# Splitting weights by two DMAs from GpSimd in place of ScalarE and GpSimd arithmetic

## The chip, the cores and the metric

The kernel runs on one core of one Trainium2 chip. The metric is device time in microseconds for one execution of the whole program; for the kernel before, three runs gave 2639.9 to 2642.7 us with a median of 2642.7.

## The reference, cut to what matters

The reference is two transformer blocks with two layers each, on 512 tokens of width 1024, all in float32. What is computed, in the order of the program:

```python
h = h + dsa_attention(rms_norm(h, g_attn_a), w_in_a, w_o_a)   # layer A: top-128 keys by an index score
h = h + sq_relu_mlp(rms_norm(h, g_mlp[0]), w_up[0], w_down[0])
h = h + fox_attention(rms_norm(h, g_attn_b), w_q_b, w_o_b, *shared_kv(h, ...))   # layer B: causal, with decay
h = h + sq_relu_mlp(rms_norm(h, g_mlp[1]), w_up[1], w_down[1])
x = rms_norm(h, g_final)
x = x + g1 * gqa_attention(modulate(rmsnorm(x), sh1, sc1), ...)   # layer C: normed heads, not causal
x = x + g2 * sq_relu_mlp_2(modulate(rmsnorm(x), sh2, sc2), mlp_w_in[0], mlp_w_out[0])
x = x + g1 * chunked_gmlp(modulate(rmsnorm(x), sh1, sc1), ...)    # gated MLP, mixing tokens of a block
x = x + g2 * sq_relu_mlp_2(modulate(rmsnorm(x), sh2, sc2), mlp_w_in[1], mlp_w_out[1])
```

The modulation vectors (sh, sc, g) come from a small product of `ada_w` with a condition vector.

## The kernel before

The residual `h` stays in SBUF as eight tiles of 128 features by 512 tokens. TensorE multiplies in `float32r`, which does not carry all bits of a float32, so every operand is split in two: a high part, rounded to float32r, and a low part, the exact difference. A product is three matmuls (`mul3`: high by high, high by low, low by high). For a tile of 128 output features and 1024 input features that is 24 matmuls of 128x512.

A weight comes in by `weight`. SP issues a plain load of 512 KB to a buffer `wr` (two of them). ScalarE copies it to `wh` in float32r, which rounds it, and a subtraction writes `wl` (three buffers of each). In most of the program VectorE subtracts, on a whole tile. Where `self.low` names GpSimd, rounding and subtraction go by two halves of 512 columns and GpSimd subtracts. This is so in layer A but for the index key's weight and the second half of the output product, for the query weights of layer B, for the query weights from the fourth on in layer C, and in `first`.

`last` and `first` stand at the boundaries of stages. `last` makes the product that completes h; its last three tiles go by halves of the tokens, so that all three weights are held to the end, while the norm of the first half (`Norm.split`) runs beside the second half. `first` is the first three tiles of the next product by the same halves: 144 matmuls of 128x256. Four stages begin with it: layer C, the MLP behind it, the gated MLP, and the last MLP.

The order of instructions is not written by hand. The program is recorded by `Sched`; `order` plays it through with assumed durations (`cost`) and gives each engine the ready instruction of lowest number, and the engines then run their queues in that order, each waiting for what its next instruction needs. A DMA is assumed to hold its engine 60 ns, then to pass through one common queue. Names in the profile are tile names: `wr`, `wh`, `wl` for weights, `xh`, `xl` for the two parts of a normed input, `st` for stacked heads, `mask` for index scores and masks in layer A, `nb` and `rs` for the shift and the factor of a softmax row, `pr` for its probabilities, `rot` and `q` for rope. All instructions have the line of the helper that emits them, L413.

Of the kernel before, what the change touches and what calls it, by code (L numbers as in the profile page):

```python
# [18 lines left out]
P = 128          # partitions, tokens of a block, features of a tile  # L19
S = 512          # tokens  # L20
D = 1024
HALVES = slice(0, S // 2), slice(S // 2, S)
KD = D // P      # feature tiles of the model width
NB = S // P      # token blocks
# [7 lines left out]
# columns of the packed per-feature vectors  # L32
# [10 lines left out]
class View:  # L43
    """a part of a tile that is not placed yet; slices and reshapes are replayed on the real one"""
# [33 lines left out]
    def bitcast(self, *a):  # L78
        """to a type of the same size"""
        return View(self.tile, self.steps + (("bitcast", a, {}),), self.box, self.flat)  # L80
# [30 lines left out]
class VPool:  # L111
    def __init__(self, sched, name, bufs, space, before, below):
        self.sched, self.name, self.bufs, self.space = sched, name, bufs, space
        self.before = before      # pools whose room it takes over
        self.below = below
        self.left = 0             # operations not emitted yet
        self.shared = None
        self.open_ = None
        self.slots = {}
# [5 lines left out]
# ns from the end of an instruction to the start of one that needs it  # L125
# [28 lines left out]
class Sched:  # L154
    """Records the program, orders each engine's instructions by a list schedule
    (ready instruction of lowest number first), then emits them in that order."""
# [29 lines left out]
    def later(self, n):  # L186
        """instructions that give way to the next n of the program"""
# [5 lines left out]
    def after(self):  # L193
        """instructions that wait for the one before them"""
# [4 lines left out]
    def record(self, eng, name, args, kw):  # L199
# [17 lines left out]
        if name == "matmul":  # L217
            # the sums of a bank one after the other
# [23 lines left out]
    def cost(o, outs, ins):  # L242
        """ns that the engine is held, and ns until the result is there"""
        ps = any(x.tile.pool.space is not None for x in ins)
        if o.name == "dma_start":
            x = (outs + ins)[0]
            return 60, 1550 + (x.box[1] - x.box[0]) * x.size * 4 / 360
# [25 lines left out]
    def order(self):  # L273
# [7 lines left out]
        parked = []               # wait for pools to be shut  # L281
# [23 lines left out]
        def room(p, q):  # L305
            if not q["free"]:
                return False
            # the first slot of a tag is its own, the others are shared by all tags of the pool
# [12 lines left out]
        while ev:  # L321
# [11 lines left out]
            while again:  # L333
                again = False
                for e, heap in ready.items():
                    while heap and busy[e] <= now:
# [15 lines left out]
                        if e == "tensor":  # L352
                            # the array runs at half its clock for a while after a pause
# [13 lines left out]
                        for s in o.succs:  # L367
                            left[s.i] -= 1
                            s.wait = max(getattr(s, "wait", 0.0), done if e == "sync" else end + LATENCY.get((e, s.eng), 130))
# [50 lines left out]
class Norm:  # L420
    """h / rms(h) * gs + sh in two parts, by halves of the tokens; twice: of h / rms(h) * g_final"""
# [8 lines left out]
    def add(self, k, c=slice(0, S)):  # L430
        """the squares of a tile of h (times the gain) to their sums"""
# [5 lines left out]
        if half and c != self.part:  # L437
            # the squares of a half take turns in the halves of a tile
# [14 lines left out]
    def split(self, c):  # L453
# [10 lines left out]
        if self.twice:  # L464
            # 1/rms(h) / rms(h / rms(h) * g) = (mean((h g)^2) + eps (mean(h^2) + eps))^-1/2
# [24 lines left out]
class Net:  # L490
    def __init__(self, ctx, tc, I, out, stop=None):
# [3 lines left out]
        self.low = None  # L495
        pool = lambda name, **kw: ctx.enter_context(self.sched.tile_pool(name, **kw))
        self.pp = pool("pp", space=PSUM)
        self.pp.shared = 4        # and a bank for each of 4 tags
# [34 lines left out]
    def weight(self, src, n):  # L533
        """src: [128, n] in DRAM; returns its high and low part"""
        w = self.t(self.wp, "wr", [P, 1024], bufs=2)
        self.nc.sync.dma_start(w[:, :n], src)
        wh = self.t(self.wp, "wh", [P, 1024], F32R)
        wl = self.t(self.wp, "wl", [P, 1024], F32R)
        if self.low is None:
            self.split(wh[:, :n], wl[:, :n], w[:, :n])  # L540
        else:
            for f in (0, n // 2):
                c = slice(f, f + n // 2)
                self.split(wh[:, c], wl[:, c], w[:, c], self.low)
# [8 lines left out]
    def fm(self, src, xh, xl, w=None):  # L553
        """one tile of 128 output features, all tokens"""
# [8 lines left out]
    def tm(self, src, xh, xl, evac, banks=("mm", "mm", "lg", "tp")):  # L563
        """a strip of output features with the tokens on partitions; src: [u, 128, kk, n]"""
# [17 lines left out]
    def squares(self, col=None):  # L582
        """sums of the squares of h (times a gain) over the features: [token, 2 * block]"""
# [16 lines left out]
    def rms(self):  # L600
        """1/rms of the columns of h: [token, block], and spread over all partitions"""
# [35 lines left out]
    def last(self, src, xh, xl, gate, norm):  # L637
        """the product that completes h, and the norm of h; the end of both goes by halves of the tokens"""
# [20 lines left out]
    def first(self, src, xh, xl):  # L659
        """the first three tiles of a product, by halves of the tokens"""  # L660
        self.low = self.nc.gpsimd
        ws = [self.weight(s.rearrange("p k n -> p (k n)"), D) for s in src]
        self.low = None
# [40 lines left out]
    def rope(self, pool, ps, cos, sin, eng, n=P, q=None, ceng=None):  # L704
        """ps * cos + (its halves of each head exchanged) * sin, in SBUF; the first n rows, repeated"""
# [14 lines left out]
    def stacks(self, pool, tag, s, bufs=None):  # L720
        """for the two heads of s: [high; low] and [low; high] along the partitions"""
# [9 lines left out]
    def doubles(self, pool, tag, s, scale):  # L731
        """for the two heads of s, scaled: [high; high] and [low; low]"""
# [13 lines left out]
    def softmax(self, pool, npr, lhs, rhs, W, masks, extra, rows, on_act=False):  # L746
        """rows of probabilities of one head, block after block; W: block of queries to its number of keys;
        lhs, rhs: pairs of operands whose products add up to the logits; rows: a factor of each row of them;
        on_act: which engine divides by the sums"""
# [669 lines left out]
```

## Time and profile before

| what | value |
|---|---|
| timed runs | 2642.7, 2639.9, 2642.7 us |
| profiled execution, span from first to last instruction | 2640.9 us, 1.8 us under the median of the timed runs (no time of its own is given beside its span) |
| TensorE busy | 2570.4 us (97%) |
| VectorE, ScalarE, GpSimd busy | 1577.0, 1159.9, 467.8 us |
| moved by DMA | 292.39 MB, mean 111 GB/s |
| mean granted clock of TensorE | 0.990 |

Shares over the whole span are means over stages with different limits: 97% for TensorE says that little idle time is there to be had, and not in which stage. TensorE's busy time also holds what a matmul takes at half clock. Where stages are compared, the table by stretches of time is the one to read: for each stretch, the time that each engine was busy in it.

### The profile page before, as it was taken

The page shows a single profiled execution, that of the slowest core. Times are in us where ns is not written, and L with a number is a line of the kernel's source. Part 1 is how long each engine was busy: PE and PEld are TensorE (multiplying, and loading weights), DVE is VectorE, ACT ScalarE, POOL GpSimd, SP SyncE. Part 2 cuts the span into 40 slices and gives each one's busy share as a digit, 9 for nine tenths or more (in the row PEclk, how much of TensorE's full clock was granted, in tenths as well). Part 3 has the DMA queues.
Part 4 walks back from the last instruction along what each step waited for, and adds up shares of the span by engine and source line. Part 5 has one row for each costly group of instructions (what it writes and reads, how often), then busy time and mean ns, then how long its engine had stood idle before and what let it go on. Part 6 is the DMA issues. An engine that isn't in the chain of part 4 may idle for free.

```text
span 2640.9 us, 34588 instructions
## 1 busy us (share of the span) xinstructions
PE 2570.4 (97%) x12998; PEld 2173.2 (82%) x12998; DVE 1577.0 (60%) x2667; ACT 1159.9 (44%) x2096; POOL 467.8 (18%) x628
## 2 busy tenths in 40 slices
PE   8989998999999998999999999999999999999999
PEld 6769787888888886888876888888998888888887
DVE  7998875455468777435698544434546654644433
ACT  5678322334477423323687433323435443523322
POOL 3773000000075000000686200000202210200000
PEclk9999999999999999999999999999999999999999
DMA  4222784223231576222211132222333332222222
GB/s 148 87 69 84 253 263 142 96 88 108 88 89 57 190 253 210 98 99 84 96 47 35 65 110 98 96 96 88 99 108 120 103 100 90 87 103 96 96 97 95
DMA packets 92056, 292.39 MB, mean 111 GB/s; under 512 B 11760, under 2 KB 16112, under 8 KB 91888
## 3 DMA queue, kind: packets, MB, share of 16 engines
q1 hardware_dynamic: 91888, 290.18, 32.8%
q8 instruction: 102, 1.67, 0.2%
q14 instruction: 66, 0.54, 0.1%
HBM read 277.28 MB, written 2.10 MB: 106 GB/s over the span
## 4 chain that ended last, share of the span: by engine, by line
PE 75%; DVE 10%; DMA 8%; ACT 3%; issue 2%; POOL 2%; SPq 0%; DVEq 0%; ACTq 0%; POOLq 0%
PE mm L413 64%; DMA adaw<-in_ada_w 7%; PE lg L413 4%; PE tp L413 4%; PE po L413 3%; DVE ada L413 2%; DVE mask L413 1%; DVE st L413 1%; ACT pr L413 1%; DVE tl L413 1%; POOL pr L413 1%; DVE m L413 1%; DVE acc L413 1%; ACT st L413 1%; ACT th L413 1%
## 5 line engine op out<-in xcount | busy, mean ns | idle before, releaser
L413 ACT ACTIVATE wh<-wr 128x1024 fp32r<-128x1024 f32 (+2 forms) x480 | 449.0, 940 | 1047.1 <-PE mm L413 865.3
L413 PE MATMUL mm<-xh,wh 128*128 128x512 f32 (+1 forms) x1640 | 627.8, 384 | 7.4 <-ACT wh L413 7.2
L413 DVE TENSOR_TENSOR wl<-wr,wh 128x1024 fp32r<-128x1024 f32 (+1 forms) x382 | 452.4, 1185 | 303.2 <-ACT wh L413 297.1
L413 PE MATMUL mm<-xh,wl 128*128 128x512 f32 (+1 forms) x1640 | 627.2, 383 | 1.3 <-DVE wl L413 0.9
L413 PE MATMUL mm<-xl,wh 128*128 128x512 f32 (+1 forms) x1640 | 627.0, 383 | 0.6 <-POOL xl L413 0.4
L413 PE MATMUL mm<-ah,wh 128*128 128x512 f32 (+1 forms) x1072 | 409.4, 382 | 16.9 <-ACT ah L413 16.9
L413 PE MATMUL mm<-al,wh 128*128 128x512 f32 (+1 forms) x1072 | 409.9, 382 | 0.7 <-DVE al L413 0.7
L413 PE MATMUL mm<-ah,wl 128*128 128x512 f32 (+1 forms) x1072 | 408.8, 381 | 1.1 <-DVE wl L413 1.1
L413 PEld LDWEIGHTS mm<-xh,wh 128*128 128x128 f32 x1640 | 311.6, 190 | 61.5 <-ACT wh L413 7.2
L413 PEld LDWEIGHTS mm<-xh,wl 128*128 128x128 f32 x1640 | 312.0, 190 | 59.7 <-DVE wl L413 3.5
L413 PEld LDWEIGHTS mm<-xl,wh 128*128 128x128 f32 x1640 | 312.5, 191 | 55.7 <-POOL xl L413 1.2
L413 PEld LDWEIGHTS mm<-ah,wh 128*128 128x128 f32 x1072 | 202.6, 189 | 58.3 <-ACT ah L413 20.0
L413 PEld LDWEIGHTS mm<-al,wh 128*128 128x128 f32 x1072 | 202.6, 189 | 41.2 <-DVE al L413 3.0
L413 PEld LDWEIGHTS mm<-ah,wl 128*128 128x128 f32 x1072 | 202.8, 189 | 39.9 <-DVE wl L413 2.0
L413 DVE SCALAR_TENSOR_TENSOR h<-mm,mod,h 128x512 f32<-128x512 f32 (+1 forms) x113 | 79.7, 707 | 260.3 <-PE mm L413 260.2
L413 POOL TENSOR_TENSOR wl<-wr,wh 128x512 fp32r<-128x512 f32 x98 | 133.1, 1368 | 144.9 <-ACT wh L413 138.4
L413 DVE SCALAR_TENSOR_TENSOR ada<-adaw,cs,ada 128x512 f32<-128x512 f32 x168 | 119.0, 748 | 43.2 <-DMA adaw<-in_ada_w 42.4
L413 DVE TENSOR_TENSOR h<-mm,h 128x512 f32<-128x512 f32 (+1 forms) x91 | 56.5, 624 | 147.0 <-PE mm L413 147.0
L413 PE MATMUL tp<-ident,pr 128*128 128x128 f32 x576 | 115.0, 278 | 7.3 <-POOL pr L413 3.4
L413 POOL TENSOR_SCALAR pr<-pr,rs 128x512 f32<-128x512 f32 (+3 forms) x168 | 110.3, 667 | 48.4 <-DVE rs L413 34.5
L413 ACT ACTIVATE ah<-a 128x512 fp32r<-128x512 f32 x128 | 80.9, 632 | 83.7 <-DVE a L413 81.6
L413 POOL TENSOR_TENSOR r<-ms,mhalf 128x2 f32<-128x2 f32 (+1 forms) x10 | 9.3, 934 | 606.9 <-DVE ms L413 545.7
(259 smaller groups left out, 4087.6 us busy)
## 6 DMA issues: line engine op xcount, KB each, us to landing
adaw<-in_ada_w SPq DMA_DIRECT2D x96, 512.0 KB, 4.5
wr<-in_w_up SPq DMA_DIRECT2D x64, 512.0 KB, 3.5
wr<-in_w_down SPq DMA_DIRECT2D x64, 512.0 KB, 3.5
wr<-in_w_in SPq DMA_DIRECT2D x64, 512.0 KB, 3.4
wr<-in_w_out SPq DMA_DIRECT2D x64, 512.0 KB, 3.5
wr<-in_w_gu SPq DMA_DIRECT2D x24, 512.0 KB, 3.5
wr<-in_w_gv SPq DMA_DIRECT2D x32, 384.0 KB, 3.0
wr<-in_w_go SPq DMA_DIRECT2D x32, 384.0 KB, 2.9
```

Of the source, the lines that this page charges most:

```text
L413: getattr(getattr(self.nc, o.eng), o.name)(*args, **kw)
```

## The change

A weight that GpSimd helped to split is now made by two DMAs that GpSimd issues. The first goes from DRAM straight to `wh` and casts float32 to float32r. ScalarE then writes minus the high part to `wl`, on the whole tile. The second DMA reads the weight from DRAM again and adds it to `wl`. Neither `wr` nor a subtraction is left there. The flag `self.low` (an engine) becomes `self.by_dma`, set at the same places. In the scheduler a DMA on GpSimd is assumed to hold its engine for 1000 ns, and what waits for a DMA is released at its landing whichever engine issued it. Comments and docstrings are removed throughout, which moves line numbers and nothing else.

```diff
@@ def cost
         if o.name == "dma_start":
             x = (outs + ins)[0]
-            return 60, 1550 + (x.box[1] - x.box[0]) * x.size * 4 / 360
+            return 1000 if o.eng == "gpsimd" else 60, 1550 + (x.box[1] - x.box[0]) * x.size * 4 / 360
@@ def order
-                            s.wait = max(getattr(s, "wait", 0.0), done if e == "sync" else end + LATENCY.get((e, s.eng), 130))
+                            s.wait = max(getattr(s, "wait", 0.0), done if o.name == "dma_start" else end + LATENCY.get((e, s.eng), 130))
@@ def weight
+        nc = self.nc
+        if self.by_dma:
+            wh = self.t(self.wp, "wh", [P, 1024], F32R)
+            wl = self.t(self.wp, "wl", [P, 1024], F32R)
+            nc.gpsimd.dma_start(wh[:, :n], src)
+            nc.scalar.activation(wl[:, :n], wh[:, :n].bitcast(F32), AF.Copy, scale=-1.0)
+            nc.gpsimd.dma_start(wl[:, :n], src, accum_op=ALU.add)
+            return wh, wl
         w = self.t(self.wp, "wr", [P, 1024], bufs=2)
-        self.nc.sync.dma_start(w[:, :n], src)
+        nc.sync.dma_start(w[:, :n], src)
         wh = self.t(self.wp, "wh", [P, 1024], F32R)
         wl = self.t(self.wp, "wl", [P, 1024], F32R)
-        if self.low is None:
-            self.split(wh[:, :n], wl[:, :n], w[:, :n])
-        else:
-            for f in (0, n // 2):
-                c = slice(f, f + n // 2)
-                self.split(wh[:, c], wl[:, c], w[:, c], self.low)
+        self.split(wh[:, :n], wl[:, :n], w[:, :n])
         return wh, wl
@@ def first (and, in the same way, layer_a, layer_b, layer_c)
-        self.low = self.nc.gpsimd
+        self.by_dma = True
         ws = [self.weight(s.rearrange("p k n -> p (k n)"), D) for s in src]
-        self.low = None
+        self.by_dma = False
```

The list schedule moves with it. On TensorE, at the boundary into layer C, this stood before (`mm` is a sum in PSUM; the first two rows end the stage before, `ah` and `al` being its input):

```order
L413 MATMUL mm_11913<-al_11677,wh_11844 128x256
L413 MATMUL mm_11913<-ah_11672,wl_11860 128x256
L413 MATMUL mm_12093<-xh_2590_12016,wh_11987 128x256
L413 MATMUL mm_12093<-xl_2598_12028,wh_11987 128x256
L413 MATMUL mm_12093<-xh_2590_12016,wl_11998 128x256
L413 MATMUL mm_12104<-xh_2590_12016,wh_12047 128x256
L413 MATMUL mm_12104<-xl_2598_12028,wh_12047 128x256
L413 MATMUL mm_12104<-xh_2590_12016,wl_12061 128x256
```

And this stands there now (`po<-ones,acc` are the sums of squares for the second half's norm):

```order
L413 MATMUL mm_11817<-al_11581,wh_11748 128x256
L413 MATMUL mm_11817<-ah_11576,wl_11764 128x256
L413 MATMUL mm_11992<-xh_2558_11919,wh_11900 128x256
L413 MATMUL mm_11992<-xl_2566_11930,wh_11900 128x256
L413 MATMUL mm_12008<-xh_2558_11919,wh_11936 128x256
L413 MATMUL mm_12008<-xl_2566_11930,wh_11936 128x256
L413 MATMUL po_12036<-ones_78,acc_11607 128x2 x2
L413 MATMUL po_12036<-ones_78,acc_11613 128x2 x2
L413 MATMUL mm_11992<-xh_2558_11919,wl_11964 128x256
```

The first matmul on a low part comes third before; now four on high parts and the norm's sums come ahead of it, and the second tile's low part is wanted only after the whole first tile.

On GpSimd, at the same place, this stood before (`rf` and `r` are the norm's inverse roots, `xl` its low parts):

```order
L413 TENSOR_TENSOR rf_11976<-ms_11969,mhalf_84 128x2
L413 TENSOR_TENSOR r_11985<-m_2646_11974,mhalf_84 128x2
L413 TENSOR_TENSOR wl_11998<-wr_11826,wh_11987 128x512 x2
L413 TENSOR_TENSOR xl_2599_12050<-y_12007,xh_2591_12038 128x256
L413 TENSOR_TENSOR wl_12061<-wr_11875,wh_12047 128x512
L413 TENSOR_TENSOR xl_2601_12091<-y_12022,xh_2593_12071 128x256
L413 TENSOR_TENSOR wl_12061<-wr_11875,wh_12047 128x512
```

And this stands there now:

```order
L413 TENSOR_TENSOR rf_11880<-ms_11873,mhalf_84 128x2
L413 TENSOR_TENSOR r_11889<-m_2614_11878,mhalf_84 128x2
L413 DMA wh_11900<-in_w_k_c 128x1024
L413 DMA wh_11936<-in_w_k_c 128x1024
L413 TENSOR_TENSOR xl_2567_11954<-y_11911,xh_2559_11941 128x256
L413 TENSOR_TENSOR xl_2569_11968<-y_11923,xh_2561_11958 128x256
L413 MEMSET bd_11986 128x2
L413 DMA wl_11964<-in_w_k_c 128x1024
L413 DMA wh_12012<-in_w_q_c 128x1024
```

Each `wh` DMA waits for the slot that a weight of the stage before holds, and each `wl` DMA for ScalarE; the other low parts of the norm stand behind them.

On GpSimd in layer A, among the first heads' softmax (`nb`) and rope (`q`, `rot`), this stood before:

```order
L413 TENSOR_TENSOR q_922<-q_922,rot_932 128x512
L413 TENSOR_TENSOR wl_1008<-wr_919,wh_974 128x512
L413 TENSOR_TENSOR q_981<-q_981,cos_109 128x512
L413 TENSOR_TENSOR rot_989<-rot_989,sin_111 128x512
L413 TENSOR_TENSOR wl_1088<-wr_956,wh_1031 128x512
L413 TENSOR_SCALAR nb_1106<-mx_1085 128x1
```

And this stands there now:

```order
L413 DMA wh_1261<-in_w_q_a 128x1024
L413 TENSOR_TENSOR q_1097<-q_1097,rot_1108 128x512
L413 TENSOR_SCALAR nb_1312<-mx_1301 128x1 x2
L413 DMA wl_1304<-in_w_q_a 128x1024
L413 TENSOR_SCALAR nb_1343<-mx_1323 128x1 x2
L413 TENSOR_TENSOR q_1282<-q_1282,cos_109 128x512
```

Where a subtraction of half a tile stood among softmax and rope, a DMA now stands, with its own wait.

## Rows read from the trace of the kernel before

**Rows 1.** Page, part 1: busy us, share of span, instructions.

```profile
PE 2570.4 (97%) x12998; PEld 2173.2 (82%) x12998; DVE 1577.0 (60%) x2667; ACT 1159.9 (44%) x2096; POOL 467.8 (18%) x628
```

**Rows 2.** By stretch: length, busy time of each engine, granted clock, DMA share, GB/s.

```profile
33.00:231.00 198.00, 178.70 (x1040) 147.84 (x1039) 189.10 (x534) 142.32 (x391) 127.99 (x174) 0.97 0.23 72
726.00:858.00 132.00, 129.73 (x751) 110.57 (x751) 100.59 (x319) 99.60 (x280) 85.23 (x158) 1.00 0.25 73
1290.00:1455.00 165.00, 155.90 (x844) 121.09 (x843) 142.26 (x268) 129.50 (x273) 126.11 (x163) 1.00 0.17 52
409.00:419.00 10.00, 5.63 (x12) 3.35 (x12) 8.89 (x12) 2.99 (x4) 0.00 (x0) 0.50 0.58 197
```

**Rows 3.** GpSimd's groups, 13 to 231 us: busy us, mean ns, idle before.

```profile
L413 POOL TENSOR_TENSOR wl<-wr,wh 128x512 fp32r<-128x512 f32 x46 | 64.0, 1402 | 51.5 <-ACT wh L413 49.8 <-PE lg L413 1.5
L413 POOL TENSOR_TENSOR q<-q,rot 128x512 f32<-128x512 f32 x10 | 13.5, 1345 | 2.0 <-DVE q L413 2.0
...
L413 POOL TENSOR_TENSOR rot<-rot,sin 128x512 f32<-128x512 f32 x10 | 13.0, 1304 | 1.7 <-DMA rot<-q 1.7
L413 POOL TENSOR_TENSOR q<-q,cos 128x512 f32<-128x512 f32 x8 | 11.2, 1406 | 4.0 <-DMA rot<-q 4.0
```

**Rows 4.** VectorE's groups, 13 to 231 us, one shape each.

```profile
L413 DVE TENSOR_TENSOR st<-q,st 64x512 fp32r<-64x512 f32 x16 | 21.2, 1326 | 0.8 <-ACT st L413 0.2
...
L413 DVE SCALAR_TENSOR_TENSOR mask<-rl,wi,mask 128x512 f32<-128x512 f32 x7 | 7.0, 1002 | 0.1
...
L413 DVE TENSOR_TENSOR st<-st,rot 128x512 f32<-128x512 f32 x5 | 5.6, 1119 | 0.1
...
L413 DVE TENSOR_TENSOR rot<-rot,sin 128x512 f32<-128x512 f32 x5 | 3.4, 680 | 0.0
...
L413 DVE SCALAR_TENSOR_TENSOR kdl<-q,kdh 64x512 fp32r<-64x512 f32 x4 | 2.7, 679 | 0.1
...
L413 DVE SCALAR_TENSOR_TENSOR xl<-h,vec,xh 128x512 fp32r<-128x512 f32 x1 | 0.7, 743 | 0.0
```

**Rows 5.** Instructions in time, boundary into layer C: start, us, [idle before].

```profile
1256.62 1.15 ACT L413 ACTIVATE wh<-wr 128x512 fp32r<-128x512 f32 x2 [2.48 <-PE mm L413]
...
1262.49 0.28 PE L413 MATMUL mm<-xh,wh 128*128 128x256 f32 x1
1262.61 0.28 PE L413 MATMUL mm<-xl,wh 128*128 128x256 f32 x1
...
1269.38 1.01 PE L413 MATMUL po<-ones,acc 128*128 128x2 f32 x4 [2.32 <-DVE acc L413]
...
1286.83 0.28 PE L413 MATMUL mm<-xh,wl 128*128 128x256 f32 x1
```

**Rows 6.** The same, first and last matmul of the three other boundaries.

```profile
1499.09 0.28 PE L413 MATMUL mm<-xh,wh 128*128 128x256 f32 x1
...
1519.98 0.28 PE L413 MATMUL mm<-xh,wl 128*128 128x256 f32 x1
...
1853.56 0.28 PE L413 MATMUL mm<-xh,wh 128*128 128x256 f32 x1
...
1874.46 0.28 PE L413 MATMUL mm<-xh,wl 128*128 128x256 f32 x1
...
2284.94 0.29 PE L413 MATMUL mm<-xh,wh 128*128 128x256 f32 x1
...
2304.60 0.28 PE L413 MATMUL mm<-xh,wl 128*128 128x256 f32 x1
```

**Rows 7.** A DMA issue on SP's queue, in time.

```profile
1.16 0.42 SPq L413 DMA_DIRECT2D wr<-in_w_ki  x1
```

**Rows 8.** DMA issues: count, KB each, median us to landing.

```profile
wr<-in_w_up SPq DMA_DIRECT2D x64, 512.0 KB, 3.5
...
wr<-in_w_gv SPq DMA_DIRECT2D x32, 384.0 KB, 3.0
...
h<-in_x SPq DMA_DIRECT2D x8, 256.0 KB, 5.2
```

More of the change, by code (lines that the diff above doesn't have):

```diff
@@ L659, in first @@
     def first(self, src, xh, xl):
-        self.low = self.nc.gpsimd
+        self.by_dma = True
         ws = [self.weight(s.rearrange("p k n -> p (k n)"), D) for s in src]
-        self.low = None
+        self.by_dma = False
         ps = [self.mm() for _ in src]
@@ L852, in layer_a @@
         kw = self.fm(I["w_ki"], xh, xl, first)
-        self.low = nc.gpsimd
+        self.by_dma = True
         r, rb = self.rms()
@@ L945, in layer_a @@
                     attend(ap, j, o1[j], 4, 3, (2, 3), False)
-                self.low = None
+                self.by_dma = False
                 self.half_out(w, o1, HALVES[1])
@@ L1017, in layer_b @@
                         with self.sched.later(50 if j else 0):
-                            self.low = nc.gpsimd
+                            self.by_dma = True
                             ps = self.fm(I["w_q_b"][j], xh, xl)
-                            self.low = None
+                            self.by_dma = False
                             s = self.t(pool, "s", [P, S])
@@ L1102, in layer_c @@
                     with self.sched.later(200 if j > 1 else 0):
-                        self.low = nc.gpsimd if j > 2 else None
+                        self.by_dma = j > 2
                         ps = q0 if j == 0 else self.fm(I["w_q_c"][j], xh, xl)
-                        self.low = None
+                        self.by_dma = False
                         s = self.rope(pool, ps, tab["q", 0], tab["q", 1], nc.gpsimd if j else nc.vector)
```

## The prediction

> **What bounds the kernel now.** I read first the page's busy shares, then busy time by stretch, then who is slowed inside the attention layers, and last the boundaries between stages. TensorE is busy for 97% of the span [rows 1], so nearly all the time is matmuls that the change leaves alone; what can move is the idle time of TensorE and the stages that another engine holds up. The table by stretches shows where those are. From 33 to 231 us (layer A) TensorE is busy 178.7 of 198 us, so 19.3 us are idle, and VectorE, busy 189.1, is the bound. In layer B (726 to 858 us) TensorE has 2.3 us idle, so next to nothing is to be had there. In layer C (1290 to 1455 us) it has 9.1 us idle of 165, with all of VectorE, ScalarE and GpSimd busy for over three quarters [rows 2].
>
> Inside layer A the reader should compare durations of one shape. The 46 `wl` subtractions take 64.0 us of GpSimd; with its three rope groups (13.5, 13.0, 11.2 us), which also read two tiles from SBUF, that makes 101.7 us, of which `wl` is 63% [rows 3]. VectorE instructions with two SBUF operands run longer here than the same work elsewhere: `st<-q,st` takes 1326 ns against 679 for `kdl<-q,kdh` of the same 64x512, `mask` 1002 against 743 for `xl`, `st<-st,rot` 1119 against 680 for `rot<-rot,sin` [rows 4]. The excess is 16 x 0.647 + 7 x 0.259 + 5 x 0.439 = 14.4 us. I put 63% of it, 9.1 us, down to the subtractions that go.
>
> At the boundaries, four of which use `first`, the weights' high and low parts live in three slots each, and the last three products of the stage before hold all of them. The first slot comes free at 1256.62, when ScalarE's wait for TensorE ends. The first matmul of layer C is at 1262.49, so the slot is free 5.9 us ahead; the 144 matmuls of `first` stand 0.12 us apart and end at 1286.95 [rows 5]. That is 17.3 us of work in 24.5 us; the rest is a wait of 2.3 us and half clock. The three other boundaries take 21.0, 21.0 and 19.8 us [rows 6]; the four together 86.3.
>
> **The change part by part.** 49 weights (24 in layer A, 8 in B, 8 in C, 9 in the three later `first`) change their way. Each loses a load on SP, two ScalarE roundings of half a tile and two GpSimd subtractions of 1.40 us, and gains a casting DMA, one ScalarE copy of the whole tile times -1, and an accumulating DMA, both issued by GpSimd.
>
> *Prices that this trace does not show.* No DMA is issued by GpSimd here, so three costs need bounds. Issue on GpSimd: not under 0.42 us, what SP's queue spends [rows 7], and I cap it at the 1.40 us of the subtraction that it replaces; the scheduler's new line assumes 1.0, which lies in the middle, and I take that. Landing of a plain 512 KB load is 3.5 us, of 384 KB 3.0 [rows 8]: 0.5 us for each 128 KB, so 2.0 us that go with size and 1.5 that do not. The cast moves the same bytes: 3.5 at best, 5.5 if its size part doubles; I take 3.5. The accumulation also has to read its destination: 3.5 at best, 5.5 with a doubled and 9.5 with a fourfold size part; I take 5.5. The copy times -1 is taken as the two half roundings in the trace, 1.15 us [rows 5].
>
> The Trainium skill ("DMA: Bandwidth & Descriptors", section "Anatomy of one DMA — SWDGE (gpsimd) path") gives a DMA from GpSimd 2.0 us plus its bytes at 436 GB/s, which for 512 KB is an estimate of 3.2 us, and makes no extra charge for accumulation. No row here shows it; by it the two landings would add up to 6.4 us instead of 9.0, and the sum would be near the first rival's.
>
> *The four boundaries.* Before, the load waited in a buffer of its own, and only rounding and subtraction had to wait for the slot. Now the load itself does. From a slot's release the chain is 1.0 + 3.5 + 1.15 + 1.0 + 5.5 = 12.2 us, so the first low part is there 12.2 - 5.9 = 6.3 us after the stage's first matmul could start. The order on TensorE has only four matmuls on high parts and the norm's sums ahead of the first that needs `wl`, so it waits. Then 140 matmuls remain, 16.8 us. The second and third slot come free 2.9 us apart (24 x 0.12), as fast as a half tile is used up, so I add no further wait. A pause of this length lowers the clock: from 409 to 419 us, with 4.4 us idle, the granted clock was 0.50 (1.2 GHz) and the 5.6 us of work there would have taken half at 2.4 GHz, 2.8 us lost [rows 2]; I take 2.5. That makes 6.3 + 16.8 + 2.5 = 25.6 us each, 102.4 in all, **16.1 us more** than 86.3. Part of the second half's norm ends sooner, as VectorE has no subtraction beside it, but it is not what the first low part waits for.
>
> *Layer A.* The 9.1 us of VectorE come back where it bounds, with TensorE's 19.3 us of idle time as the cap. Against it: GpSimd's and ScalarE's queues are in order, so `wl`'s DMA waits on GpSimd for ScalarE's copy, and that one on ScalarE for the first landing; behind them stand `nb` and rope, for which ScalarE's exponentials and the score products wait. I count **8 us gained**, within 0 and 13.
>
> *Layer C.* 5 weights free 10 x 1.40 us of GpSimd and spend 10 x 1.0 on issue: 4 us of an engine that is one of three in the way. **1 us gained.** *Layer B:* 2.3 us of idle time at most, **nothing**. *ScalarE:* two halves become one tile, no more than 0.2 us each, off the path. *SP* loses 49 issues and was not waited for.
>
> *The start.* Two casting loads of 512 KB go out at once beside the eight loads of h, which land after 5.2 us [rows 8]; before, the w_qi loads stood behind them in SP's queue. h later by 0 to 3 us, the time of 1 MB at 0.5 us for 128 KB being 4: **1 us lost**.
>
> Sum: 16.1 - 8 - 1 + 1 = +8.1 us, a span of 2649.0. The profiled span of 2640.9 lies 1.8 us below the median of the timed runs, 2642.7, so I predict **2651 us**.
>
> **The rivals.** *First: the two DMAs are as quick as a plain load, and the end is faster.* Issue 0.42, landing 3.5 each: the chain is 9.0 us, the first low part comes 3.1 us late, a boundary takes 3.1 + 16.8 + 1 = 20.9 us, 2.7 us less than before over the four. Layer A then gains 12, as queues do not hold up each other and VectorE's other stretched forms, too, find an emptier GpSimd, and layer C 4: -19 us, 2624. For it: with 5.9 us ahead, a chain of up to about 10 us costs a boundary nothing, since it has 4 us of slack of its own. Against it: nothing in the trace reads a destination and writes it at a plain load's speed. The mechanism decides where both landings together fall under about 7.5 us.
>
> *Second: the accumulation is far slower, and the in-order queues hand the delay on.* Issue 1.4, cast 5.5, accumulation 9.5: the chain is 19.0 us, a boundary 13.1 + 16.8 + 2.5 = 32.4, 129.6 in all or 43 more. A slot's round of 19.0 us and 24 matmuls at 0.24 makes 8.2 us for each weight with three slots, close to the 9.6 us that layer A has for each of its 24 (231 us), so its gain turns into some 12 us lost; start and layer B add 3 each: +61, 2704. Against it: DMA engines are idle for three quarters of layer A (share 0.23, [rows 2]).
>
> *Third: nothing moves*, since layer A's gain and the boundaries' loss cancel: 2643. It is the near end of the forecast and not a mechanism of its own.
>
> **How the numbers follow.** Forecast 0.47, spread from 2641 to 2665; first rival 0.28; second 0.25. What a measurement of this kernel can tell from no change is 0.2%, 5.3 us. Faster than 2637.4: nearly all of the first rival, 0.27. Within: the near end of the forecast and a bit of the first rival, 0.18. Slower than 2648: 0.55. The range leaves about a tenth on each side: 2628 to 2695; the forecast's own is 2641 to 2665.
>
> **What would show it.** Right: at each boundary TensorE waits 5 to 7 us for `wl` behind the first four matmuls on `xh`, followed by half clock; the `wl` DMAs land 5 to 6 us after issue, the `wh` ones after 3 to 4; in layer A `st<-q,st` falls from 1326 ns towards 900 and TensorE's idle time shrinks. The boundary step is wrong if `first` ends in under 22 us. Layer A's step is wrong if VectorE's durations fall and the stage does not get shorter, with GpSimd waiting at its DMAs for ScalarE or for slots. The prediction falls as a whole if landings lie outside 3 to 7 us, or if issuing holds GpSimd much longer than 1.4 us.

## The result and the profile after

The changed kernel takes 2706.9 us (median of 4 runs, 2704.1 to 2710.0) against 2641.3 us for the kernel before on the same chip (median of 4): 1.025 times as long, 95% interval 1.0234 to 1.0267. The profiled execution spans 2705.2 us, 64.3 more than before. I had predicted 2651 us within 2628 to 2695: the right sign, an eighth of the size, and outside the range. The second rival's 2704 was the nearest number.

The page's busy shares answer to [rows 1]. TensorE is busy 22 us longer with the same 12998 matmuls, while the mean granted clock falls from 0.990 to 0.978; GpSimd and VectorE are busy 66 and 24 us less.

```profile
PE 2592.3 (96%) x12998; PEld 2195.1 (81%) x12998; DVE 1553.4 (57%) x2667; ACT 1157.8 (43%) x2047; POOL 402.1 (15%) x628
```

I split the span at the first sums of squares of each norm (`po<-ones,acc`), which TensorE does in both kernels. The stretches of the changed kernel, in order, from the start through layer A, the first MLP, layer B, its MLP and layer C, up to the second MLP's norm (columns as in [rows 2]):

```profile
0.00:24.90 24.90, 12.78 (x34) 8.81 (x34) 12.29 (x19) 15.73 (x24) 4.27 (x13) 0.93 0.88 276
24.90:293.30 268.40, 239.17 (x1409) 205.99 (x1407) 212.89 (x600) 169.53 (x417) 106.79 (x179) 0.92 0.52 123
293.30:660.60 367.30, 358.69 (x1603) 294.48 (x1602) 219.07 (x287) 115.79 (x148) 2.02 (x2) 0.99 0.49 158
660.60:920.40 259.80, 253.72 (x1451) 218.48 (x1450) 164.93 (x412) 157.94 (x362) 79.00 (x161) 1.00 0.39 105
920.40:1282.00 361.60, 351.58 (x1595) 290.47 (x1594) 213.54 (x282) 112.04 (x142) 1.48 (x1) 0.98 0.49 160
1282.00:1536.10 254.10, 230.69 (x1299) 190.02 (x1298) 182.26 (x339) 163.28 (x329) 133.56 (x191) 0.95 0.27 69
```

The same stretches of before, split alike, are 21.2, 248.9, 369.2, 255.2, 360.0 and 237.3 us; layer A and layer C among them:

```profile
21.20:270.10 248.90, 229.21 (x1397) 195.32 (x1398) 227.22 (x599) 171.95 (x441) 137.63 (x182) 0.97 0.28 91
1254.50:1491.80 237.30, 225.81 (x1298) 185.17 (x1297) 183.26 (x339) 163.09 (x337) 147.69 (x191) 0.99 0.19 61
```

Beside my terms:

| term | predicted | measured |
|---|---|---|
| start | +1 | +3.7 |
| layer A | -8 | +19.4 |
| layer B | 0 | +4.6 |
| layer C without its boundary | -1 | +14.9 |
| the four boundaries | +16.1 | +22.2 |
| all the rest | 0 | -0.5 |
| sum | +8.1 | +64.3 |

The table is the reading that matters: the boundaries came out about as worked out, and the attention layers, which I had down as a gain, lost 39 us.

**The prices.** Medians from issue to landing over the whole run, columns as in [rows 8]:

```profile
wh<-in_w_q_a POOLq DMA_DIRECT2D x8, 512.0 KB, 4.4
wl<-in_w_q_a POOLq DMA_DIRECT2D x8, 512.0 KB, 5.6
...
wh<-in_w_in POOLq DMA_DIRECT2D x6, 512.0 KB, 3.9
wl<-in_w_in POOLq DMA_DIRECT2D x6, 512.0 KB, 8.0
wh<-in_w_qi POOLq DMA_DIRECT2D x4, 512.0 KB, 6.5
h<-in_x SPq DMA_DIRECT2D x8, 256.0 KB, 7.3
```

Accumulations land 5.4 to 5.7 us after issue in the layers (5.5 predicted), and casts 3.7 to 6.5 (3.5 predicted). Those of `w_in`, at the second and the last boundary, have a median of 8.0. The packet records say why casts scatter. GpSimd's DMAs go through one queue, in order. A cast issued while the queue is empty (17 of 49) has its first packet 1.3 us later and its last 3.5 us after issue; one issued while an accumulation runs (21 of 49) has its first packet 4.05 us after issue and its last 5.7. A 4 KB packet takes 174 ns when it casts and 328 ns when it accumulates. By the Trainium skill ("DMA: Bandwidth & Descriptors", "Anatomy of one DMA — SWDGE (gpsimd) path") the estimate is 3.2 us, with no price of its own for an accumulation. That is near the 3.5 us of a cast alone and does not hold for an accumulation, whose last packet comes 5.1 us after issue when the queue is empty; the measurement decides. The Trainium skill ("DMA: Bandwidth & Descriptors", "SWDGE vs HWDGE vs iDMA") says that only one such queue is allocated; the trace agrees, with 4.05 us against 1.3 to the first packet.

**A boundary.** Into layer C, GpSimd, ScalarE and TensorE in time (start, us, idle before), answering to [rows 5]:

```profile
1284.62 0.64 POOL L413 DMA_DIRECT2D wh<-in_w_k_c  x1 [0.28 <-issue]
...
1288.48 1.04 ACT L413 ACTIVATE wl<-wh 128x1024 fp32r<-128x1024 f32 x1
...
1289.83 0.91 POOL L413 DMA_DIRECT2D wl<-in_w_k_c  x1
...
1289.98 0.28 PE L413 MATMUL mm<-xh,wh 128*128 128x256 f32 x1
...
1291.40 0.39 PE L413 MATMUL mm<-xh,wh 128*128 128x256 f32 x1 [1.02 <-DMA wh<-in_w_k_c]
...
1294.12 0.82 PE L413 MATMUL po<-ones,acc 128*128 128x2 f32 x4 [2.21 <-DVE acc L413]
1295.19 1.01 PE L413 MATMUL po<-ones,acc 128*128 128x2 f32 x4 [0.25 <-DVE ms L413]
1296.07 0.56 PE L413 MATMUL mm<-xh,wl 128*128 128x256 f32 x1
...
1316.19 0.28 PE L413 MATMUL mm<-xh,wl 128*128 128x256 f32 x1
```

The cast goes out at 1284.62, the copy ends at 1289.52, the accumulation goes out at 1289.83 and lands 5.5 us later, at 1295.30: 10.7 us after the cast's issue (12.2 predicted), 5.3 us behind the stage's first matmul (6.3 predicted). TensorE uses it at 1296.07, 6.1 us behind that matmul. It does not stand still for the low part here: it waits 1.0 us for the second high part and 2.2 us for VectorE's sums of the norm, which stand ahead of the low part in its order, and their matmuls last past the landing. At the three other boundaries the wait for `wl` is there, 4.0, 4.5 and 4.0 us, after 1.0 to 1.6 us for a high part; the second one:

```profile
1544.76 0.39 PE L413 MATMUL mm<-xh,wh 128*128 128x256 f32 x1 [1.00 <-DMA wh<-in_w_in]
...
1549.22 0.58 PE L413 MATMUL mm<-xh,wl 128*128 128x256 f32 x1 [3.96 <-DMA wl<-in_w_in]
```

The low parts there are used 5.9, 6.6 and 9.4 us behind the first matmul. Into layer C the matmuls behind it are 0.21 us apart instead of 0.12 for a while; from 1295 to 1316 us the granted clock is 0.85. From the first to the last of the 144 matmuls, 0.12 us added as before, the four boundaries take 26.3, 26.4, 26.7 and 29.0 us, 108.4 against 86.3 [rows 5, 6].

**Inside layer A.** What TensorE waits for from 13 to 294 us (in total, times, longest):

```profile
PE lg L413 <- DVE st L413: 10.2, 8, 3.5
PE mm L413 <- DMA wl<-in_w_q_a: 7.0, 3, 5.1
PE mm L413 <- DMA wl<-in_w_qi: 4.7, 1, 4.7
PE tp L413 <- ACT pr L413: 4.0, 4, 2.1
PE po L413 <- ACT th L413: 2.9, 3, 2.2
PE mm L413 <- DMA wl<-in_w_o_a: 1.4, 1, 1.4
```

Three of the six are late low parts, 13.1 us, and none of these stood in the trace before. VectorE's relief is there, as the 46 subtractions of [rows 3] are gone: `st<-q,st` fell from 1326 ns [rows 4] to 1041, `mask<-rl,wi,mask` of 512 columns from 1002 to 748, and VectorE, busy for 227 of the layer's 249 us before, is busy for 213 of 268: it no longer bounds it. Idle time is only half of the layer's loss: by the two rows of the layer above, TensorE is idle for 29.2 us (19.7 before) and busy for 10.0 us more with nearly as many matmuls, at a granted clock of 0.92 against 0.97. One of the waits, in time:

```profile
101.53 0.85 POOL L413 DMA_DIRECT2D wl<-in_w_q_a  x1 [6.73 <-ACT wl L413]
102.37 0.58 POOL L413 DMA_DIRECT2D wh<-in_w_q_a  x1
106.48 0.56 POOL L413 DMA_DIRECT2D wh<-in_w_q_a  x1 [3.53 <-PE mm L413]
...
110.43 1.07 ACT L413 ACTIVATE wl<-wh 128x1024 fp32r<-128x1024 f32 x1 [3.35 <-DMA wh<-in_w_q_a]
...
110.68 1.29 POOL L413 TENSOR_TENSOR q<-q,cos 128x512 f32<-128x512 f32 x1 [3.65 <-DMA rot<-q]
...
113.17 0.89 POOL L413 DMA_DIRECT2D wl<-in_w_q_a  x1
...
118.71 0.79 PE L413 MATMUL mm<-xh,wl 128*128 128x512 f32 x1 [5.07 <-DMA wl<-in_w_q_a]
```

The cast issued at 102.37 stands in the DMA queue behind the accumulation of 101.53, so ScalarE's copy starts only at 110.43, 8.1 us after the cast's issue. GpSimd has by then begun rope, which waited 3.65 us for its own small transfers (`rot<-q`, 64 KB, lands after 3.4 us here, 2.0 before), and issues the accumulation behind it at 113.17. TensorE stands still for 5.07 us.

### The profile page after: what moved, and what is told of

It is laid out like the page before. It is cut to its first block, busy times and chain, and to the rows that moved or that the text cites. A ratio compares the mean times of both kernels' runs of the same rounds, so it can differ in the third digit from the quotient of the medians.

```text
span 2705.2 us, 34567 instructions
## 1 busy us (share of the span) xinstructions
PE 2592.3 (96%) x12998; PEld 2195.1 (81%) x12998; DVE 1553.4 (57%) x2667; ACT 1157.8 (43%) x2047; POOL 402.1 (15%) x628
## 4 chain that ended last, share of the span: by engine, by line
PE 72%; DMA 12%; DVE 7%; ACT 4%; issue 4%; POOL 1%; SPq 1%; DVEq 0%; POOLq 0%; ACTq 0%
PE mm L413 63%; DMA adaw<-in_ada_w 6%; PE lg L413 4%; PE tp L413 3%; PE po L413 2%; DVE ada L413 2%; DMA rot<-q 1%; ACT pr L413 1%; DVE st L413 1%; DMA wl<-in_w_in 1%; SPq L413 1%; DVE wl L413 1%; DVE tl L413 1%; ACT th L413 1%; DMA wl<-in_w_q_a 0%
## 5 line engine op out<-in xcount | busy, mean ns | idle before, releaser
L413 ACT ACTIVATE wh<-wr 128x1024 fp32r<-128x1024 f32 (+1 forms) x382 | 389.5, 1020 | 1035.2 <-PE mm L413 870.1
L413 PEld LDWEIGHTS mm<-ah,wh 128*128 128x128 f32 x1072 | 203.2, 190 | 58.4 <-ACT ah L413 19.8
L413 DVE TENSOR_TENSOR al<-a,ah 128x512 fp32r<-128x512 f32 x128 | 88.2, 691 | 46.5 <-ACT ah L413 46.4
L413 DVE TENSOR_TENSOR tl<-tp,th 128x512 fp32r<-128x512 f32 (+1 forms) x224 | 103.5, 493 | 13.9 <-ACT th L413 12.4
```

Of the source, the lines that this page charges most:

```text
L413: getattr(getattr(self.nc, o.eng), o.name)(*args, **kw)
```

## The experiments

All were run against the kernel before on the same chip; ratios are to it. Stage times are from one trace each, split as above. Where the instructions of layer A stand in the same order, its length still differs between traces: 265.1, 268.4 and 268.9 us (e2, the change, e3), 253.7 and 259.2 (e9, e13), 247.7 to 249.0 (e1, before, e14). So a stage's difference of less than some 5 us is not told from chance. The ways of `weight` were made selectable for each of its four places (`first`, A, B, C); "old" is the way before.

**e1: `first` alone.**

```diff
+WAYS = {"first": "dma", "A": "old", "B": "old", "C": "old"}
```

> The two DMAs only where a stage starts with first (12 weights in layer C, the two MLPs and the gated one); the 37 other weights of layers A, B and C as before. All theories agree that the four boundaries alone come out: they took 109.2 us after against 86.3 before, so some 2664 us (before + 23). If the waits of the attention layers had come from the boundaries (a later start that shifts their order), it would be nearer 2690.

Measured 2670.8 us, 1.0115 (1.0099 to 1.0130). The boundaries took 29.3, 26.3, 25.3 and 26.9 us to the ends of their last matmuls, 107.8 (the 109.2 and 86.3 above count the ends and the starts; by ends before is 86.9). So they cost 21 us, as all theories had it, and layer C lost 6.6 more behind its boundary, which none had. The traced execution, at 2664.9 us, was the fastest of the four; its stages do not show where the median's other 6 us are.

**e2: the attention layers alone.**

```diff
+WAYS = {"first": "old", "A": "dma", "B": "dma", "C": "dma"}
```

> The reverse of the run before: the two DMAs in the attention layers alone, first as before. If losses simply add, 2641 + 65 - 23 = 2683 us: start +3.7, layer A +19, layer B +5, layer C +13 to +15. My prediction on record had -8 for these stages together, 2633.

Measured 2674.7 us, 1.0135 (1.0119 to 1.0150). It is 8 us under the expected 2683, as layer C lost less. Stages: start +3.7, A +16.2, B +8.4, C +4.7. The excesses of e1 and e2 add up to 2.5%, the whole change. Of the 14.9 us of layer C without its boundary, 6.6 appear with `first` alone (e1) and 4.7 with its own five weights; the other 3.6 are less than the spread of a stage.

**e3: layer A alone.**

```diff
+WAYS = {"first": "old", "A": "dma", "B": "old", "C": "old"}
```

> The two DMAs for the 24 weights of layer A alone. Adding: +3.7 at the start and +19.4 in the layer, 2664 us. VectorE's st<-q,st stays near 1040 ns as after the change, so the relief is there, and the layer is longer all the same.

Measured 2662.8 us, 1.0092 (1.0075 to 1.0109); start +4.1, layer A +19.9, `st<-q,st` 1029 ns. As expected, and the base for e5 to e8 and e13.

**e4: the plan told the landings.**

```diff
-            return 1000 if o.eng == "gpsimd" else 60, 1550 + ...
+            if o.eng == "gpsimd":
+                return (890, 5600) if "accum_op" in o.kw else (600, 4400)
...
-                            done = hw + o.extra
+                            done = now + o.extra if e == "gpsimd" else hw + o.extra
```

> The changed kernel, but the list schedule is told what the trace of the changed kernel shows: GpSimd held 0.60 us by the casting and 0.89 by the accumulating DMA, landing 4.4 and 5.6 us after the issue (it assumed 1.0 and about 3.7). Theory 1 (the order was made for landings that come too early, so GpSimd waits at its DMAs with other work queued behind): GpSimd's waits at wh and wl in layer A fall from some 67 us to under 30, layers A and C win back 15 to 30 us, 2677 to 2692. Theory 2 (three slots and a chain of about 12 us for each weight cannot supply the layers at their speed, whatever the order): within 6 us of 2707.

Measured 2702.3 us, 1.0229 (1.0211 to 1.0247): theory 2's number. Layer A stayed at +19.3, and GpSimd's waits at its DMAs did not shrink. But these landings are medians; they do not say that a cast behind an accumulation starts later. e9 says it.

**e5: two casts, no chain.**

```diff
             nc.gpsimd.dma_start(wh[:, :n], src)
-            nc.scalar.activation(wl[:, :n], wh[:, :n].bitcast(F32), AF.Copy, scale=-1.0)
-            nc.gpsimd.dma_start(wl[:, :n], src, accum_op=ALU.add)
+            nc.gpsimd.dma_start(wl[:, :n], src)
```

> Layer A alone by DMA, but the low part is filled by a second casting DMA that waits for nothing but its slot: no copy times -1, no accumulation (the low parts are left out, wl holds the rounded weight). Theory S (supply: the chain cast, copy, accumulate, with accumulating packets of 328 ns against 174 and the next cast behind them in the same DMA queue, delivers low parts late): the layer falls under before's, since the VectorE relief that I predicted is there without the late low parts; 2631 to 2642 us against 2663 with the full chain. Theory Q (GpSimd's other work, held behind its DMA instructions that wait for slots, is what costs): most of the loss stays, 2652 or more.

Measured 2635.4 us, 0.998 (0.997 to 0.999). Layer A is 241.6 us, 7.3 shorter than before (the start is 2.5 longer):

```profile
23.70:265.30 241.60, 225.42 (x1395) 193.22 (x1396) 210.59 (x598) 148.31 (x395) 99.21 (x178) 0.97 0.44 132
```

TensorE's waits there hold no `wl` any more:

```profile
PE lg L415 <- DVE st L415: 7.2, 7, 2.8
PE tp L415 <- POOL pr L415: 2.1, 3, 1.0
PE po L415 <- DVE acc L415: 1.4, 1, 1.4
```

So the gain that I had priced at 8 us can be had once low parts come in time. That all of the 7.3 is VectorE's relief is not shown: e5 also takes from ScalarE its work on these weights (busy 148 us in the layer, 172 before), and the planner makes another order for it. GpSimd's waits do not cost by themselves: here it waits 62.7 us at casts for slots, and the layer is the shortest of all. That speaks against theory Q as the main cause.

**e6: the chain without the accumulation.** As e3, but the second DMA overwrites the copy:

```diff
-            nc.gpsimd.dma_start(wl[:, :n], src, accum_op=ALU.add)
+            nc.gpsimd.dma_start(wl[:, :n], src)
```

> Layer A alone by DMA, the chain as in the change, but the second DMA writes the rounded weight over the copy instead of adding to it (the low parts are left out). If the slow accumulating packets and what queues behind them are the bulk of the loss: the second DMA lands 3.5 us after issue instead of 5.1 and casts start 1.3 us after issue instead of 4; 2648 to 2654 us. If the serial waits (slot, cast, ScalarE, second DMA) are the bulk: 2658 to 2664.

Measured 2646.1 us, 1.0018 (1.0007 to 1.0029), below both ranges. Layer A is 254.6 us:

```profile
23.80:278.40 254.60, 236.06 (x1407) 203.31 (x1406) 211.29 (x600) 168.76 (x417) 98.69 (x179) 0.93 0.43 130
```

Up to the end of the layer every engine has the instructions of e3 in the same order, but for the accumulation itself, so the 14.3 us from 268.9 to 254.6 are what accumulating costs instead of casting (18.5 us by the medians of the runs). The 13.0 us from e5 to e6 (241.6 to 254.6) are the serial step through ScalarE together with another order; how much the step costs by itself is not shown. TensorE's idle time in e6, 18.5 us, is under before's 19.7: what e6 loses against before is busy time, 6.9 us at a granted clock of 0.93. How long the queue is held can be read from its share of the 16 engines' time, 20 to 290 us; the changed kernel, then e5 (casts alone):

```profile
q0 software_dynamic: 6586, 23.96, 40.9%
```

```profile
q0 software_dynamic: 6324, 23.02, 27.8%
```

Nearly as many bytes take 1.4 times the engines' time for each MB when half of them are accumulated.

**e7: the accumulation alone.**

```diff
+            nc.scalar.activation(wh[:, :n], w[:, :n], AF.Copy)          # w: loaded by SP, as before
+            nc.scalar.activation(wl[:, :n], wh[:, :n].bitcast(F32), AF.Copy, scale=-1.0)
+            nc.gpsimd.dma_start(wl[:, :n], src, accum_op=ALU.add)
```

> Layer A alone, all computed: SP loads the weight into its own buffer as before, ScalarE rounds it into the high part and copies that times -1, GpSimd issues only the accumulating DMA. The load is again ahead of the slot, the DMA queue holds accumulations alone. Theory S: the chain from the slot is 1.1 + 1.1 + 0.9 + 5.1 = 8.2 us instead of 12, most late low parts go and the VectorE relief stays: 2636 to 2648 us. Theory Q: as many accumulating DMAs wait for ScalarE on GpSimd's queue as before, 2655 to 2665.

Measured 2658.1 us, 1.0061 (1.0042 to 1.0081): a miss for theory S, and inside theory Q's range. The start is as before (-0.7), but layer A is +18.7. Its trace shows ScalarE waiting 30.2 us for slots at the rounding and GpSimd 77.6 us for the copies: the wait for the slot moved onto ScalarE, and TensorE still waits for `wl` four times longer than 1 us. A shorter chain on paper was not enough. This run has an order of its own; whether that or the waits of ScalarE's and GpSimd's queues cost more is not shown, and the chain with a fitting plan was not tried in this layer.

**e8: a fourth pair of slots.**

```diff
+            if self.by_dma == "A" and self.nw % 4 == 3:
+                wh = self.t(self.wp, "wr", [P, 1024], F32R, 2)
+                wl = self.t(self.wp, "wr", [P, 1024], F32R, 2)
```

> Layer A alone by DMA, with a fourth pair of slots (every fourth weight keeps its two parts in the two load buffers, which the layer does not use otherwise). Theory S with three slots as the limit: casts start a slot's round earlier, TensorE's waits for wl (10 us in the layer) go and half clock with them; 2642 to 2652 us. Theory Q: GpSimd waits less for slots but as long for ScalarE's copies, 2655 to 2662.

Measured 2670.6 us, 1.0114 (1.0097 to 1.0131): both theories' numbers missed, on the slow side. Of the waits for low parts of `w_q_a` one of 1.7 us is left (in a `wr` buffer), but `lg` waits 19.0 us for VectorE's stacks, one of them 5.7, and the layer's last weights find their load buffers taken (5.1). A fourth pair made in this way does not help. Since it takes the load buffers and changes the order, it does not show that slots are not the limit; and it shows that the layer can be long with few waits for low parts.

**e9: a plan that knows the queue.** e4's second place, with a queue of its own:

```diff
+                            if e == "gpsimd":
+                                sw = max(sw, now + (1600 if "accum_op" in o.kw else 1300)) + o.extra   # 3450 or 2050
+                                done = sw + 250
```

> The changed kernel with a better plan than e4: the list schedule treats GpSimd's DMAs as one queue in order, 1.3 or 1.6 us from issue to the first packet, then 2.05 us for a cast and 3.45 us for an accumulation, one after the other, as the trace shows. If the order is at fault (copies and accumulations placed too early in front of other work), layers A and C win back 10 us or more: 2690 or less. If the supply itself is late (the chain on the slots and the one DMA queue), the order has little to give: 2697 to 2707, like e4 (2702).

Measured 2693.9 us, 1.0207 (1.0191 to 1.0222). The total is between the expectations, but the stages are not: layer A falls from +19.4 to +4.8, layer C with its boundary from +16.8 to +12.5, layer B rises from +4.6 to +14.7.

**e13: the same plan in layer A alone** (e3 with e9's lines).

> Layer A alone by DMA with e9's plan (one DMA queue in order). In e9 layer A was 253.7 us against 268.4 with the change's own plan and 249.0 before. If that was the plan, it comes out again: layer A 252 to 256 and the start +1, 2643 to 2650 us. If it came from what lies around layer A in e9, the layer is 262 to 269 as in e3, 2655 to 2663.

Measured 2650.6 us, 1.0029 (1.0019 to 1.0039), just past the upper end. The layer is 259.2 us, between the two forecasts and 5.5 longer than in e9 with the same order; the start is +0.5:

```profile
21.70:280.90 259.20, 235.29 (x1412) 199.66 (x1412) 213.66 (x600) 168.51 (x418) 106.47 (x180) 0.95 0.54 131
```

TensorE's longest waits for `wl` there are down to 2.0 us. Of the 24 us that start and layer lose in e3, 13 come back with the order alone and 11 stay. For this layer theory 2 of e4, that the order does not matter, is wrong.

**e10: two casts everywhere.**

```diff
+WAYS = {"first": "nocopy", "A": "nocopy", "B": "nocopy", "C": "nocopy"}
```

> All 49 weights with two casting DMAs that wait for the slot alone (no copy, no accumulation; the low parts are left out). If the chain behind the slot is the whole of the loss, at the boundaries as in layer A: the chain is under 6 us, so the boundaries fall back to 84 to 92 us (before 86.3, after 109.2), layer A keeps its -7, layers B and C come to within 4 us of before: 2628 to 2645. If other costs of DMAs on GpSimd (contention with the loads, issue) matter there: 2655 or more.

Measured 2650.8 us, 1.0038 (1.0025 to 1.0050), 6 above the range. The boundaries fell to 20.0, 19.8, 19.8 and 24.3 us (83.9), layer A to -5.1, layer C with its boundary to +0.6 (+5.2 behind the boundary); layer B is at +9.4 and makes the miss. There TensorE waits twice, 2.8 and 2.9 us, for the query's high part (`lg` behind `qh`), with half clock behind. So 55 of the change's 64 us go with copy and accumulation and with the order that the planner made for them, and layer B's loss is something else.

**e11 and e12: fewer weights by DMA.** With e9's plan, from the fifth `w_q_a` on and the first half of `w_o_a` (12 weights), or that half alone (8):

```diff
                 for j in range(KD):
+                    if j == 4:
+                        self.by_dma = "A"
```

> A version that could beat both: by DMA only the 12 weights of layer A that are not waited for at once (w_q_a from the fifth on, and the first half of w_o_a), with e9's plan; the others as before. TensorE's waits for wl of the changed kernel lay in the first half of the layer (at 22, 96, 107 and 119 us) and once at 216. If they stay away and half of the VectorE relief is kept: 2636 to 2639 against 2641. If late low parts appear here too: 2645 to 2655.

> The smaller version of e11: by DMA only the eight weights of the first half of w_o_a, whose products fill gaps and are waited for last. Expected 2637 to 2642, no difference that can be measured or 3 us faster; slower only if accumulations hold the copies of q in front of rope (64 KB, 2.0 us before, 3.4 us after the change).

Measured 2640.7 us, 1.0002 (0.9994 to 1.0010), and 2639.0 us, 0.9996 (0.9986 to 1.0006): no difference. Neither beats the kernel before.

**e14: the accumulation alone at the boundaries** (e7's lines for `first`, with e9's plan).

> The boundaries alone, all computed, with the load ahead of the slot again: SP loads into its own buffer, ScalarE rounds and copies times -1, GpSimd issues the accumulating DMA only. By the boundary step of my prediction: 1.05 + 1.05 + 5.05 and some 0.5 between them is 7.6 us from the slot against 5.9 us that it is free ahead, so 1.7 us late instead of 6.1; each boundary 1.7 + 16.8 + 1 to 2.5 of clock, 78 to 84 us for four (before 86.3, by both DMAs 107.8 in e1), 2633 to 2644. If ScalarE's norm work or the landing next to the following loads (8.0 us for the last MLP) sets it instead: 92 us or more, 2646 or later.

Measured 2671.2 us, 1.0109 (1.0094 to 1.0125): the rival's side. The boundaries took 31.0, 25.6, 29.1 and 26.3 us, 112.0. At the second one TensorE waits 2.0 us for the first `wl`, close to my 1.7, but the others wait 5.2, 4.6 and 5.6. The first accumulations of the four boundaries land 8.7, 5.8, 8.4 and 7.8 us after issue, while SP's queue moves 1.9, 0.8, 1.2 and 1.0 MB beside them; two that go out to an empty queue with nothing beside them land after 5.3 and 5.2. I had priced them alone. The 8.0 us of the last MLP that I had taken for the same effect have another cause: from 2335 to 2360 us of the changed kernel no load of SP moves, and its accumulations stand behind casts and each other.

## Why the prediction was wrong

**Prices: right, alone.** Issue holds GpSimd 0.53 to 0.93 us in nearly all cases (1.0 taken), a cast alone takes 3.5 to its last packet, an accumulation 5.1 (landing after 5.4 to 5.7 in the layers), the copy 1.05. I priced each DMA as if the queue were empty. They share it in order, and 21 of the casts pay 2.2 us more for that.

**The boundaries: right mechanism, undersized by 6 us.** For a first use 6.3 us late, 6.1, 5.9, 6.6 and 9.4 were measured. The 6.1 into layer C is in part luck: the low part was there after 5.3, and the norm's sums, ahead of it in the order, held TensorE. I counted those sums and the four matmuls on high parts as time without waits; they wait 1.0 to 1.6 us for the second weight's high part and, at two boundaries, 2.2 and 1.7 us for VectorE. Two things were missing, of about the same size: the last boundary has three casts ahead of the accumulation, which lands 8.2 us after issue; and what follows the first low part takes 3.0 to 3.8 us more than its matmuls at full clock, not 2.5.

**Layer A: the step that failed.** It says "I count 8 us gained, within 0 and 13", from VectorE's relief, and takes off about a microsecond for copies and DMAs that wait for each other. Without copy and accumulation the layer did get 7.3 shorter (e5); as the change has them it got 19.4 longer. What the step left out is the boundary's own chain: each of the 24 weights of the layer goes from its slot through cast, copy and accumulation too, and TensorE waits for low parts that come late. Between e5 and e3 that is 27 us: 14 by accumulating, which e6 shows with nothing else changed, and 13 by the serial copy and another order together. Seen from the other side, more than half of the net loss, 13 of 24 us, is due to an order made for landings that do not happen (e13); the two accounts overlap and do not add up. I also put the clock at nothing in this layer: 10 us of its loss are not idle time but more busy time, at a lower granted clock. I had worked the chain out for the boundaries and put it into the second rival for the layer, at a chance of 0.25, arguing against it with idle DMA engines (share 0.23). That argument was the mistake: the engines' share went to 0.52 (0.28 before in the same stretch), still half idle, and a cast behind an accumulation still has its first packet only 4.05 us after issue. The test I named, durations falling and the stage not getting shorter, is what the trace shows.

**Layer C: failed, and the cause is open in part.** I predicted -1 and measured +14.9 behind the boundary; when copy and accumulation go, +5.2 are left there (e10). Late low parts are not the greatest wait: for `wl` of `w_q_c` TensorE waits 2.7 us, behind GpSimd's `pr` 6.6 us in all, against 1.5 before. The longest of these, 3.6 us, has GpSimd's rope and the issue of a `wl` DMA just ahead of `pr`. How much is GpSimd's queue and how much the low parts, no run separates. From the waits of the changed kernel, 1278 to 1543 us:

```profile
PE tp L413 <- POOL pr L413: 6.6, 6, 3.6
PE mm L413 <- DMA wl<-in_w_q_c: 2.7, 1, 2.7
```

and of the kernel before, 1250 to 1499 us:

```profile
PE tp L413 <- POOL pr L413: 1.5, 3, 0.5
```

**Layer B and start.** I had nothing and +1; they cost 4.6 and 3.7. The start has h landing after 7.3 us instead of 5.2 [rows 8] and a wait of 4.7 us for the first `wl` of `w_qi`. With e9's plan the start loses only 0.5 (e9, e13). Layer B stays open: it lost 8.4 in e2, 14.7 in e9, and 9.4 in e10 with neither accumulation nor copy, so these do not explain it. That the load now waits for its slot, and the first query with it, is argued from the waits for `qh`, not shown.

**The rivals.** The second came out at the right total for partly wrong reasons: no accumulation took 9.5 us in the layers, issue took 0.9 and not 1.4, boundaries cost half of its +43, and the slot's round, on which it based layer A, is neither shown nor excluded (e8); the 231 us that it divides by are the end of a window, and the layer has 249. The first decides below 7.5 us for both landings; measured are 8.6 at least, 3.5 and 5.1. Of the signs that I named, landings outside 3 to 7 us did occur, up to 8.2.

## What to carry to other kernels

When a load into a buffer of its own, followed by arithmetic, becomes a DMA straight into the working slot, the load's latency moves behind the slot's release; charge that chain to every weight of the stage, not just where the pipeline starts. DMAs of one queue have to be priced as a queue, and a planner that orders engines has to be told so, or it places the waiting instructions in front of others; that won back half of layer A's loss and made layer B longer (e9), so the new order has to be measured too. Removing a contention that bounds an engine is worth its time only if the new supply is in time: test that bound first, with a cheap stand-in such as e5.

## What the runs showed that I had not expected

- An accumulating packet of 4 KB takes 328 ns on the queue, a casting one 174; a 512 KB accumulation needs 3.45 us from first to last packet, a cast 2.1.
- Small transfers on SP's queue slow down beside them: `rot<-q` (64 KB) lands after 3.4 us instead of 2.0 in layer A.
- With SP's loads beside it an accumulation lands later: 7.8 to 8.7 us after issue beside 1.0 to 1.9 MB in e14, against 5.2 and 5.3 with nothing beside it.
- Half of what layer A lost is no wait of TensorE at all: it stood idle for 9.5 us more and was busy for 10.0 us more, at a granted clock of 0.92 against 0.97.
